# More borders in the side work, another order for the first pair of products, and side work that rests while operands are split

## The chip, the cores and the metric

The kernel runs on one core of a Trainium2 chip. The metric is device time in microseconds of one execution; the profile adds one profiled execution with its span from the first to the last instruction. Engines are named as the profile names them: PE (matrix products), PEld (its weight loads), DVE, ACT and POOL (elementwise work), SP (the queue that issues the DMAs).

## The reference

One step of a decoder layer for 1024 prompt tokens and 8 samples of 4 tokens (1056 token columns), width 1024, all in float32:

```python
sh1, sc1, g1, sh2, sc2, g2 = split(silu(c) @ w_ada + b_ada, 6)   # per sequence
h = ln(x) * (1 + sc1) + sh1
qm, km, vm, ig, fg, og, qa, ka, va, gm, ga = split(h @ w_in + b_in)
hm = ln(mlstm(qm, km, vm, ig, log_sigmoid(fg))) * norm_w * sigmoid(og)   # 4 heads, chunks of 128
ha = sliding_window_attention(qa, ka, va)                        # 16 heads, 4 kv heads, window 128
x = ln(ALPHA * x + g1 * ((sigmoid(gm) * (hm @ w_branch_m) + sigmoid(ga) * (ha @ w_branch_a)) @ w_out))
h2 = ln(x) * (1 + sc2) + sh2
x = ln(ALPHA * x + g2 * ((gelu(conv_a(h2 @ w_up)) * conv_b(h2 @ w_up)) @ w_down))
```

Outputs are x for prompt and samples and the new states: mLSTM matrix, normaliser and maximum, the last 128 keys and values, the last two columns before the convolution.

## The kernel before

**Products.** Each float32 operand is split in two parts of a shorter format (hi, a cast on ACT; lo, a subtraction on DVE) and a product is hi·hi + hi·lo + lo·hi: three matmuls for each 128-deep piece. `group` (lines 440 to 449) makes one 128-row block of a product for one of three column tiles (384, 384 and 288 columns, `TT`): eight pieces, 24 matmuls, in one of three PSUM banks `L`. `Stream` loads the weights of a block two blocks ahead and splits them one block ahead (`win.ahead_of`).

**Stages.** First the norm of x and four blocks for the branch gate (`direct(0)` to `direct(3)`). Then ten pairs of blocks in a form with seven half-size products instead of eight (`fast`, `Pair`, products numbered 1 to 7 at line 1445). Then 28 blocks and the gate rows for the heads (`direct`, line 1545). Then the branch stages: eight blocks of `w_branch_m` (line 1667), called BM0 to BM7 here, and eight of `w_branch_a` (line 1685), BA0 to BA7. Then `w_out`, the up and down products and the end.

**Side work.** The gate rows (`gate_rows`), the mLSTM heads (`mlstm`), the attention groups (`swa`) and the remaining modulation vectors (`ada_rest`) are Python generators in a queue `sides`. A `yield` is a border between two steps. `group` calls `pulse(nt / 800)` after each piece; `pulse` adds that times `rate[0]` to a counter and runs one step for each whole unit. So a block of three tiles is worth 8 · (0.48 + 0.48 + 0.36) = 10.56 units, a step comes each 1/rate units, and the order of all instructions on each engine is fixed when the program is built. `finish_sides` runs what is left with no products between. `mlstm` sets the rate to `RATE_M`, `swa` to `RATE_S`.

**Places that the change touches.**
- `fast`: `t1_split` (line 1354) splits the operands of product 5 on ACT and DVE before the first product. Products 1 and 2 read the same split weights `pa`; product 6 reads those of `ps[0]`, split in the last step of `first_pair` (`step(2)`, lines 1403 and 1404).
- `gate_rows` (line 642): exponentials on ACT, scans and elementwise work on DVE, in 13 steps.
- `mlstm` (line 802): 11 steps for the chunks, then the sample part. Copies into `C0T` (line 930), a border, products on them (line 937). Then `norm_apply` into `hs` (line 761 through line 979), a border, transposes of `hs`.
- `swa` (line 1043): two steps that split the queries (line 1064), then 13 steps of a software pipeline; its first step computes the biases `bg`, the scores (line 1184) and the sample scores (line 1086), a later one copies scores (lines 1189 and 1190).
- The last `direct` block (qa, block 7) sets the rate to 0, reads the finished heads back from DRAM (`raw_pieces`, line 1303) and splits them tile by tile into the operands of BM (`refill`, lines 1313 and 1314). The rate goes back to `RATE_S` at line 1639, ahead of BM0.
- BM7 reads the attention outputs back (16 pieces of 192 KB, later 8 of 144 KB), refills the operands, and puts `ada_rest` in the queue: a load of four tiles of 512 KB (line 231), three borders, 32 matmuls (line 241), and so on eight times.

Of the kernel before, what the change touches and what calls it, by code (L numbers as in the profile page):

```python
# [30 lines left out]
TT = [(0, 384), (384, 384), (768, 288)]  # L31
NSLOT = 43

RATE_G, RATE_M, RATE_S, RATE_A = 0.44, 0.54, 0.46, 0.46
RATES = [0.442, 0.395, 0.35, 0.45, 0.463, 0.495, 1.0, 0.7, 0.417]


# [67 lines left out]
def hybrid_step(ctx: ExitStack, tc: tile.TileContext, I, O):  # L105
# [48 lines left out]
    rate = [0.26]  # L154
# [487 lines left out]
    def gate_rows():  # L642
        fi, lf = rows_f["i"], rows_f["f"]
        na, rm, bb, Q, M, t5 = (slot(name="gr") for _ in range(6))
        r = slice(0, 4)
        V.memset(Q, 0.0)
        V.memset(rm[r], 1.0)
        V.memset(rm[r, 0:SEQ:128], 0.0)
        V.memset(rm[r, SEQ:TOK:4], 0.0)
        V.scalar_tensor_tensor(na[r], lf[r], -1.0, lf[r], op0=OP.mult, op1=OP.max)  # L650
        yield
        yield
        A.activation(na[r], na[r], AF.Exp, scale=-1.0)
        A.activation(na[r], na[r], AF.Ln, bias=1.0)
        yield
        V.scalar_tensor_tensor(lf[r], lf[r], 0.0, na[r], op0=OP.min, op1=OP.subtract)
        V.tensor_tensor_scan(bb[r], rm[r], lf[r], 0.0, op0=OP.mult, op1=OP.add)
        g = Q[r]
        V.tensor_tensor(g, fi[r], bb[r], op=OP.subtract)
        yield  # L660
        d0 = na
        V.memset(d0[r, :SEQ], 0.0)
        V.tensor_copy(d0[r, 128:SEQ:128], bb[r, 127:SEQ - 1:128])
        V.memset(d0[r, SEQ:], BIG)
        V.memset(d0[r, SEQ:TOK:4], -BIG)
        gs = t5[r, SEQ:]
        V.tensor_copy(gs, Q[r, SEQ:])
        V.tensor_tensor(gs[:, 0:32:4], gs[:, 0:32:4], m0, op=OP.max)
        V.tensor_tensor_scan(M[r, :SEQ], d0[r, :SEQ], Q[r, :SEQ], 0.0, op0=OP.add, op1=OP.max)
        V.tensor_tensor_scan(M[r, SEQ:], d0[r, SEQ:], gs, -BIG, op0=OP.min, op1=OP.max)  # L670
        mp = tiny([4, 16], "mp", 1)
        MT = tiny([4, 16], "MT", 1)
        bT = tiny([4, 16], "bT", 1)
        dec = tiny([4, 16], "dec", 1)
        V.tensor_copy(MT[:, 0:8], M[r, 127:SEQ:128])
        V.tensor_copy(MT[:, 8:16], M[r, SEQ + 3:TOK:4])
        V.tensor_copy(bT[:, 0:8], bb[r, 127:SEQ:128])
        V.tensor_copy(bT[:, 8:16], bb[r, SEQ + 3:TOK:4])
        V.tensor_tensor(mnew, bT, MT, op=OP.add)
        V.memset(mp[:, 0:1], 0.0)  # L680
        V.tensor_copy(mp[:, 1:8], mnew[:, 0:7])
        V.tensor_copy(mp[:, 8:16], m0)
        V.tensor_tensor(dec, mp, MT, op=OP.subtract)
        S.dma_start(mD, M[r])

        def bc(x):
            return (x[:, 0:8][:, :, None].to_broadcast([4, 8, 128]), x[:, 8:16][:, :, None].to_broadcast([4, 8, 4]))

        t = lf
        p8, s8 = bc(MT)  # L690
        V.tensor_tensor(chunks(t[r, :SEQ]), chunks(Q[r, :SEQ]), p8, op=OP.subtract)
        V.tensor_tensor(to3(t[r, SEQ:]), to3(Q[r, SEQ:]), s8, op=OP.subtract)
        t = fi
        p8, s8 = bc(mp)
        V.tensor_tensor(chunks(t[r, :SEQ]), p8, chunks(M[r, :SEQ]), op=OP.subtract)
        V.tensor_tensor(to3(t[r, SEQ:]), s8, to3(M[r, SEQ:]), op=OP.subtract)
        V.tensor_tensor(t5[r], bb[r], M[r], op=OP.add)
        for _ in range(4):
            yield
        A.activation(dec, dec, AF.Exp)  # L700
        S.dma_start(dD, dec)
        A.activation(Q[32:36], lf[r], AF.Exp)
        A.activation(Q[64:68], fi[r], AF.Exp)
        A.activation(Q[96:100], t5[r], AF.Exp, scale=-1.0)
        S.dma_start(aD, Q[64:68])
        S.dma_start(decb.rearrange("p a b -> p (a b)"), dap(dD, 0, [[0, 128], [1, 64]]))
        S.dma_start(O["p_m"].rearrange("a b c -> (a b) c").rearrange("a c -> c a"), mnew[:, 7:8])
        S.dma_start(O["s_m"].rearrange("a b c -> (a b) c").rearrange("a c -> c a"), mnew[:, 8:16])
        for _ in range(4):
            yield  # L710
        for i in range(8):
            transpose(pd(i), Q[:, i * 128:(i + 1) * 128])
        transpose(PE_[:32, :128], Q[:, SEQ:])
        for i in range(2):
            V.tensor_copy(colQ[:, 4 * i:4 * i + 4],
                          PD[i].rearrange("p (i q x) -> p i q x", i=4, q=4)[:, :, :, 0:4])
        V.tensor_copy(colQ[:32, 8], PE_[:32, :128].rearrange("p (q x) -> p q x", q=4)[:, :, 0:4])
        drop(fi, lf, na, rm, bb, Q, M, t5)
        yield
# [82 lines left out]
    def mlstm(h):  # L802
# [117 lines left out]
        for q4 in range(2):  # L920
            for half_ in range(2):
                p = ((PF, PG) if q4 else PD)[half_]
                for bi in range(2):
                    b = 4 * q4 + 2 * half_ + bi
                    for vb in range(2):
                        o = bi * 256 + vb * 128
                        transpose(p[:, o:o + 128], C0[vb][:, b * 128:(b + 1) * 128])
                eng = A.copy if half_ else V.tensor_copy
                eng(c0v[q4][:, 2 * half_:2 * half_ + 2, 0:256], p.rearrange("p (b x) -> p b x", b=2))
            V.tensor_copy(c0v[q4][:, :, 256:257], n0T.rearrange("p (b h) -> p b h", h=4)[:, 4 * q4:4 * q4 + 4, h:h + 1])  # L930
            if q4:
                go_ahead(h + 1)
            yield
        for r in range(2):
            for j in range(4):
                b = 4 * r + j
                T.matmul(PE_[32 * j:32 * j + 32, :257], qm[:, b, :], c0v[r][:, j, :], start=r == 0, stop=r == 1,
                         tile_position=(0, 32 * j))
# [38 lines left out]
        yield  # L977
        hs = tiny([32, 256], "hs", 1, "isb")
        norm_apply(hs, num[:, :256], nrm, 32)
        yield  # L980
        for i in range(2):
            transpose(PG[:, i * 32:(i + 1) * 32], hs[:, i * 128:(i + 1) * 128], 32)
# [60 lines left out]
    def swa(g):  # L1043
        rate[0] = RATE_S
        p, o = g // 2, g % 2
# [14 lines left out]
        for j in range(2):  # L1060
# [5 lines left out]
                G.tensor_copy(qs[me, :, 2 * j + hh, :], to3(zq[j][a, SEQ:]))  # L1066
            yield
        drop(*zq)
        bg = tiny([128, 4, 128], "bg", 1)
        for i in range(4):  # L1070
            V.tensor_scalar(bg[:, i, :], cst[:, C_DELTA:C_DELTA + 128], slope(4 * g + i), None, op0=OP.mult)
# [60 lines left out]
        for s in range(13):  # L1132
# [39 lines left out]
            n = s  # L1172
# [95 lines left out]
    def ada_rest():  # L1268
        todo = [(ca, cb, 256 * s) for ca, cb in ((3, 4), (2, 5)) for s in range(4)]
        w = ada_load(*todo[0])  # L1270
        for i, (ca, cb, f0) in enumerate(todo):
            for _ in range(3):
                yield
            ada_mm(w)
            if i + 1 < len(todo):
                w = ada_load(*todo[i + 1])
            sa = ada_copy()
            yield
            ada_sel(sa, f0)
            ada_put(ca, cb, f0)  # L1280
# [70 lines left out]
            V.tensor_tensor(t3_ops[kp][1], e[:, :, 1, :], t3_ops[kp][0].bitcast(F32), op=OP.subtract)  # L1351
            yield

    def t1_split():

        for kp in range(4):
            hi, lo = (quarters(t)[:, :, 1, :] for t in acts[2 * kp])
            x = quarters(hf[2 * kp])[:, :, 0, :]
            A.copy(hi, x)
            V.tensor_tensor(lo, x, hi.bitcast(F32), op=OP.subtract)  # L1360
        drop(hf[4], hf[6])

    def operand(p, kp, g):

# [114 lines left out]
    def fast(pairs, at_end):  # L1479

        prev = None
        t1_split()
        for n, pr in enumerate([*pairs, None]):
            nxt = pairs[n + 1] if n + 1 < len(pairs) else None
            for pos, p in enumerate((1, 3, 6, 2, 7, 4, 5)):
                who = prev if p == 3 else pr
                if who is not None:
                    for g in range(2):
# [7 lines left out]
                if pos == 0:  # L1496
                    if n:
                        pr.step(2)
                elif pos == 1:
                    pr.step(3)  # L1500
                    pr.step(4)
                elif pos == 2 and nxt is not None:
                    nxt.load()
                    if n in (2, 4):
                        kept_cache(n // 4)
                elif pos == 3:
                    drop(*pr.pa)
                elif pos == 4 and nxt is not None:
                    nxt.step(0)
                elif pos == 5:  # L1510
                    drop(pr.pq)
                    if nxt is not None:
                        nxt.step(1)
                elif pos == 6:
                    drop(*pr.ps[0])
# [120 lines left out]
        return t  # L1636

    nxt = gate_load("gm", 0)
    rate[0] = RATE_S
    mD2 = [dram.tile([128, TOK], F32, name=f"moutD{j}") for j in range(8)]  # L1640

    def m_out(j, t):
# [8 lines left out]
    for j in range(8):  # L1651
# [11 lines left out]
        for ti, (t0, nt) in enumerate(TT):  # L1663
            ps = lbank()
            if ti == (not j):
                win.ahead_of(BM + j)
            group(ps, win.parts[BM + j], acts, TT[ti])
            V.tensor_tensor(gt[:, t0:t0 + nt], ps[:, :nt], gt[:, t0:t0 + nt], op=OP.mult)
            if j == 7:
# [558 lines left out]
```

## Time and profile before

| | us |
|---|---|
| median of 3 runs (lowest, highest) | 2037.14 (2032.62, 2042.41) |
| the profiled execution | 2039.19 |
| its span | 2037.3 |
| PE busy | 1950.2 |
| DVE busy | 1116.8 |
| ACT busy | 738.2 |
| mean granted PE clock | 0.981 |

PE is busy almost all the time, so the time between its matmuls and the time at a granted clock of 0.5 are what there is to look for. A row of the waits names who waited, for whom, the sum, the count and the longest. A timeline row has start, duration, engine, line, operation and, in brackets, the idle time before it with what ended it.

### The profile page before, as it was taken

To read this page: it belongs to the slowest core of one execution; us is meant where nothing else is said; L and a number is where in the kernel's file an instruction comes from. 1 tells how busy PE (TensorE), PEld (TensorE's weight loads), DVE (VectorE), ACT (ScalarE), POOL (GpSimd) and SP (SyncE) were. 2 spreads that over 40 slices of the span, in tenths; PEclk is the share of its full clock that TensorE was granted. 3 is DMA by queue.
4 is the path that set the end of the run, shared out by engine and by line. 5 is a ranking of instruction groups with operands and counts; after the bars stand their busy time and mean duration, and the time that the engine had idled before them with its cause. 6 is when DMAs were issued, how large, how long until landed. Compare 5 with 4: busy or idle time off the path is not lost. (4 is left out here: it accounts for less than half of the span.)

```text
span 2037.3 us, 32186 instructions
## 1 busy us (share of the span) xinstructions
PE 1950.2 (96%) x12837; PEld 1851.3 (91%) x12837; DVE 1116.8 (55%) x2374; ACT 738.2 (36%) x1530; POOL 303.8 (15%) x592
## 2 busy tenths in 40 slices
PE   6999999998999999899799999999999999999996
PEld 4999998988898889888689999999999999999995
DVE  5666665555655462654334355474545454646579
ACT  5431224443443563545211345443222222223331
POOL 2000000422440321123000153100000000000007
PEclk9999999999999999899899999999999999999998
DMA  9224343464343213333884323111211111111533
GB/s 292 85 91 149 96 128 67 148 171 135 92 123 95 64 43 100 116 117 106 284 292 146 94 93 120 46 34 47 62 33 48 47 47 48 47 40 48 195 127 127
DMA packets 222942, 216.03 MB, mean 106 GB/s; under 512 B 9745, under 2 KB 199873, under 8 KB 222761
## 3 DMA queue, kind: packets, MB, share of 16 engines
q1 hardware_dynamic: 222013, 213.38, 34.1%
q8 instruction: 100, 1.64, 0.3%
q10 hardware_dynamic: 780, 0.61, 0.1%
q14 instruction: 49, 0.40, 0.1%
HBM read 164.12 MB, written 51.87 MB: 106 GB/s over the span
## 5 line engine op out<-in xcount | busy, mean ns | idle before, releaser
L448 PE MATMUL L<-mhi,whi 128*128 128x384 f32 (+1 forms) x1248 | 408.5, 327 | 4.8 <-DVE r L1807 3.0
L448 PE MATMUL L<-mhi,wlo 128*128 128x384 f32 (+1 forms) x1248 | 404.0, 324 | 0.0
L448 PE MATMUL L<-mlo,whi 128*128 128x384 f32 (+1 forms) x1248 | 403.5, 323 | 0.1
L448 PE MATMUL L<-hhi,whi 128*128 128x384 f32 (+1 forms) x1120 | 375.8, 336 | 0.1
L448 PE MATMUL L<-hhi,wlo 128*128 128x384 f32 (+1 forms) x1120 | 367.1, 328 | 2.6 <-DVE wlo L426 2.6
L448 PE MATMUL L<-hlo,whi 128*128 128x384 f32 (+1 forms) x1120 | 366.8, 328 | 0.0
L426 DVE TENSOR_TENSOR wlo<-wraw,whi 128x1024 fp32r<-128x1024 f32 (+1 forms) x128 | 150.1, 1173 | 328.6 <-ACT whi L422 328.1
L448 PEld LDWEIGHTS L<-mhi,whi 128*128 128x128 f32 x1248 | 235.7, 189 | 6.6 <-DVE r L1807 3.3
L448 PEld LDWEIGHTS L<-mlo,whi 128*128 128x128 f32 x1248 | 235.7, 189 | 0.3 <-DVE mlo L1780 0.3
L448 PEld LDWEIGHTS L<-mhi,wlo 128*128 128x128 f32 x1248 | 235.3, 189 | 0.0
L448 PEld LDWEIGHTS L<-hhi,whi 128*128 128x128 f32 x1120 | 215.5, 192 | 6.7 <-issue 4.8
L448 PEld LDWEIGHTS L<-hhi,wlo 128*128 128x128 f32 x1120 | 215.1, 192 | 2.9 <-DVE wlo L426 2.9
L448 PEld LDWEIGHTS L<-hlo,whi 128*128 128x128 f32 x1120 | 215.8, 193 | 0.4
L1852 ACT ACTIVATE u<-L,vT 128x384 f32<-128x384 f32 (+1 forms) x132 | 71.9, 546 | 379.7 <-PE L L448 379.6
L448 PE MATMUL L<-ahi,whi 128*128 128x384 f32 (+1 forms) x432 | 139.6, 323 | 0.0
L448 PE MATMUL L<-alo,whi 128*128 128x384 f32 (+1 forms) x432 | 139.3, 323 | 0.0
L448 PE MATMUL L<-ahi,wlo 128*128 128x384 f32 (+1 forms) x432 | 139.3, 322 | 0.0
L422 ACT CAST whi<-wraw 128x1024 fp32r<-128x1024 f32 (+1 forms) x128 | 128.2, 1003 | 28.4 <-DMA wraw<-in_w_up 19.6
L1865 DVE SCALAR_TENSOR_TENSOR y<-u,vT,y 128x1023 f32<-128x1023 f32 (+3 forms) x92 | 113.7, 1235 | 2.5
L1875 POOL COPY ucol<-u 128x2 f32<-128x2 f32 x44 | 10.4, 236 | 631.2 <-ACT u L1852 631.2
L2021 DVE TENSOR_TENSOR facc<-L,facc 128x384 f32<-128x384 f32 (+1 forms) x120 | 62.7, 522 | 58.4 <-PE L L448 58.3
L448 PEld LDWEIGHTS L<-ahi,whi 128*128 128x128 f32 x432 | 81.2, 188 | 0.0
(579 smaller groups left out, 3586.5 us busy)
## 6 DMA issues: line engine op xcount, KB each, us to landing
wada<-in_w_ada SPq DMA_DIRECT2D x44, 512.0 KB
wraw<-in_w_up SPq DMA_DIRECT2D x44, 512.0 KB
wraw<-in_w_in SPq DMA_DIRECT2D x32, 512.0 KB
fraw<-in_w_in SPq DMA_DIRECT2D x20, 512.0 KB
wraw<-in_w_down SPq DMA_DIRECT2D x24, 384.0 KB
vD<-fdst SPq DMA_DIRECT2D x8, 528.0 KB
ogD<-fdst SPq DMA_DIRECT2D x8, 528.0 KB
v<-vD SPq DMA_DIRECT2D x8, 528.0 KB
```

The costliest lines, as they stand in the source:

```text
L422: A.copy(hi[:, :n], t[:, :n])
L426: V.tensor_tensor(lo[:, :n], t[:, :n], hi[:, :n].bitcast(F32), op=OP.subtract)
L448: T.matmul(ps[:, :nt], x[:, c], y[:, t0:t0 + nt], start=i == 0, stop=i == last)
L1852: A.activation(u[:, t0:t0 + n], ps[:, :n], AF.Identity, bias=b)
L1865: V.scalar_tensor_tensor(y[:, f:b], u[:, f - d:b - d], w[i], y[:, f:b], op0=OP.mult, op1=OP.add)
L1875: G.tensor_copy(aux["ucol"][:, c, 0:2], u[:, SEQ - 2:SEQ])
L2021: V.tensor_tensor(fx, ps[:, :nt], fx, op=OP.add)
```

## The change

Six borders (`yield`) are added and one is taken out in `gate_rows`, `mlstm` and `swa`, and five in a row stand before the first product of `ada_rest`; the four rates go up by 2 to 4%. The first pair's products come in the order 1, 2, 6, 7, 4, 5 instead of 1, 6, 2, 7, 4, 5 (product 3 belongs to the pair before and the first pair has none), and its `t1_split` is cut in three parts. The rate goes back to `RATE_S` one tile later, after BM0's first tile.

```diff
-RATE_G, RATE_M, RATE_S, RATE_A = 0.44, 0.54, 0.46, 0.46
+RATE_G, RATE_M, RATE_S, RATE_A = 0.46, 0.56, 0.475, 0.47
...
         V.tensor_tensor_scan(bb[r], rm[r], lf[r], 0.0, op0=OP.mult, op1=OP.add)
+        yield
...
         V.tensor_tensor(gs[:, 0:32:4], gs[:, 0:32:4], m0, op=OP.max)
+        yield
         V.tensor_tensor_scan(M[r, :SEQ], d0[r, :SEQ], Q[r, :SEQ], 0.0, op0=OP.add, op1=OP.max)
...
+        yield
         t = lf
...
-        for _ in range(4):
+        for _ in range(3):
             yield
         A.activation(dec, dec, AF.Exp)
...
             if q4:
                 go_ahead(h + 1)
             yield
+        yield
         for r in range(2):
...
         norm_apply(hs, num[:, :256], nrm, 32)
+        yield
         yield
...
         drop(*zq)
+        yield
         bg = tiny([128, 4, 128], "bg", 1)
...
         w = ada_load(*todo[0])
+        for _ in range(5):
+            yield
...
-    def t1_split():
+    def t1_split(kps):
 
-        for kp in range(4):
+        for kp in kps:
...
-        drop(hf[4], hf[6])
+            if kp > 1:
+                drop(hf[2 * kp])
...
-        t1_split()
+        t1_split([0])
...
-            for pos, p in enumerate((1, 3, 6, 2, 7, 4, 5)):
+            for pos, p in enumerate((1, 3, 6, 2, 7, 4, 5) if n else (1, 3, 2, 6, 7, 4, 5)):
...
                 if pos == 0:
                     if n:
                         pr.step(2)
+                    else:
+                        t1_split([1])
                 elif pos == 1:
                     pr.step(3)
                     pr.step(4)
+                    if not n:
+                        t1_split([2, 3])
...
     nxt = gate_load("gm", 0)
-    rate[0] = RATE_S
...
             if ti == (not j):
                 win.ahead_of(BM + j)
+                if not j:
+                    rate[0] = RATE_S
```

## Rows read from the trace of the kernel before

**Rows 1.** The page: busy time of PE, and the granted clock of PE in 40 slices of the span, in tenths.

```profile
PE 1950.2 (96%) x12837; PEld 1851.3 (91%) x12837; DVE 1116.8 (55%) x2374; ACT 738.2 (36%) x1530; POOL 303.8 (15%) x592
...
PEclk9999999999999999899899999999999999999998
```

**Rows 2.** The waits of PE over the whole span: who waited for whom, us in total, times, longest.

```profile
PE PE L241 <- DMA wada<-in_w_ada: 11.8, 4, 10.4
PE PD L1184 <- DVE scr L1190: 8.1, 3, 6.0
PE PE L937 <- DVE C0T L930: 6.2, 5, 1.9
PE PD L1445 <- ACT fhi L1403: 5.5, 1, 5.5
PE PG L197 <- ACT hs L761: 4.8, 4, 1.7
...
PE L L448 <- DVE wlo L426: 2.6, 1, 2.6
PE PD L1184 <- DVE q L1064: 2.4, 3, 0.8
...
PE PE L832 <- DVE wx L843: 2.3, 3, 1.5
```

**Rows 3.** Stretches around those waits: start and end, length, busy time of PE, PEld, DVE, ACT and POOL with their instructions, then the granted clock of PE, the DMA share and GB/s.

```profile
98.00:110.00 12.00, 5.92 (x29) 5.40 (x28) 10.79 (x17) 7.17 (x12) 0.00 (x0) 0.72 0.26 83
348.00:353.00 5.00, 4.81 (x19) 4.81 (x20) 1.36 (x2) 1.55 (x3) 0.00 (x0) 0.66 0.84 47
419.00:428.00 9.00, 6.82 (x38) 4.73 (x37) 7.68 (x20) 3.48 (x6) 0.12 (x1) 0.81 0.81 221
...
551.00:558.00 7.00, 5.89 (x32) 4.12 (x33) 6.58 (x18) 1.54 (x3) 0.00 (x0) 0.76 0.79 244
613.00:620.00 7.00, 7.00 (x51) 4.98 (x50) 3.04 (x12) 0.96 (x2) 0.00 (x0) 1.00 0.60 72
646.00:656.00 10.00, 9.07 (x46) 8.68 (x45) 5.29 (x19) 2.57 (x12) 0.00 (x0) 0.66 0.21 52
719.00:728.00 9.00, 8.09 (x47) 7.61 (x45) 5.49 (x20) 2.90 (x13) 0.00 (x0) 0.81 0.23 60
813.00:824.00 11.00, 10.25 (x54) 10.00 (x54) 5.41 (x19) 2.53 (x5) 0.00 (x0) 0.69 0.24 73
843.00:851.00 8.00, 6.49 (x25) 6.49 (x26) 5.18 (x26) 4.83 (x22) 1.04 (x1) 0.57 0.50 157
904.00:913.00 9.00, 8.89 (x52) 8.66 (x51) 5.23 (x19) 2.13 (x11) 0.00 (x0) 0.81 0.21 64
985.00:1001.00 16.00, 5.15 (x25) 1.94 (x26) 5.32 (x11) 4.36 (x9) 0.00 (x0) 0.68 1.08 361
```

**Rows 4.** Timeline of the first pair: on PE the first matmul of product 6 and the first of product 7, on ACT and DVE the splits of product 6's weights.

```profile
104.15 0.59 PE L1445 MATMUL PD<-thi,fhi 128*128 128x264 f32 x1 [5.48 <-ACT fhi L1403]
105.55 0.59 PE L1445 MATMUL PD<-thi,flo 128*128 128x264 f32 x1 [0.59 <-DVE flo L1404]
...
113.16 0.28 PE L1445 MATMUL L<-th,fhi 128*128 128x264 f32 x1
...
103.06 1.03 ACT L1403 CAST fhi<-fsum 128x1024 fp32r<-128x1024 f32 x1
...
108.49 1.22 DVE L1404 TENSOR_TENSOR flo<-fsum,fhi 128x1024 fp32r<-128x1024 f32 x1
```

**Rows 5.** Timeline around the gate rows: the cast of a block's weights on ACT, the second scan and the subtraction for the same weights on DVE.

```profile
334.16 1.04 ACT L422 CAST whi<-wraw 128x1024 fp32r<-128x1024 f32 x1
...
338.50 0.91 DVE L662 MEMSET gr<- 4x1024 f32 x1 [0.16 <-issue]
...
346.93 1.21 DVE L426 TENSOR_TENSOR wlo<-wraw,whi 128x1024 fp32r<-128x1024 f32 x1
```

**Rows 6.** Timeline of PE where the fourth attention group begins: the sample scores.

```profile
906.06 1.96 PE L1086 MATMUL PG<-qs,kcT 64*128 64x16 f32 x16
```

**Rows 7.** Timeline of BM0's begin: its first matmul and the wait on PE, on ACT the last cast of the refill, on DVE the copies of scores that PE waits for.

```profile
834.12 0.34 PE L448 MATMUL L<-hhi,whi 128*128 128x384 f32 x1
...
844.51 0.58 PE L1184 MATMUL PD<-khi,q 128*128 128x256 f32 x1 [6.01 <-DVE scr L1190]
...
841.65 0.43 ACT L1313 CAST hhi<-raw 128x288 fp32r<-128x288 f32 x1 [1.06 <-DMA raw<-hD]
...
844.01 0.77 DVE L1190 COPY_PREDICATED scr<-cst,PD 128x256 f32<-128x256 int32 x2 [1.44 <-ACT scr L1189]
```

**Rows 8.** BM7: the evacuations of BM6's last two tiles and BM7's first on DVE (each begins as its tile ends), the wait on PE, SP's issues, and the casts of the third tile's refill.

```profile
972.85 0.56 DVE L1668 TENSOR_TENSOR gate<-L,gate 128x384 f32<-128x384 f32 x1 [3.64 <-PE L L448]
975.99 0.46 DVE L1668 TENSOR_TENSOR gate<-L,gate 128x288 f32<-128x288 f32 x1 [2.58 <-PE L L448]
980.18 0.56 DVE L1668 TENSOR_TENSOR gate<-L,gate 128x384 f32<-128x384 f32 x1 [2.60 <-PE L L448]
...
995.53 1.06 PE L241 MATMUL PE<-wada,cT 128*32 128x256 f32 x2 [10.41 <-DMA wada<-in_w_ada]
...
992.98 7.35 SPq L1303 DMA_DIRECT2D raw<-haD  x8
...
1002.55 2.77 ACT L1313 CAST hhi<-raw 128x288 fp32r<-128x288 f32 x8
```

## The prediction, made before the changed kernel ran

> **What bounds the kernel now.** I read the page first, then the waits of PE, then the granted clock around each wait, then timelines there. PE is busy 1950.2 of 2037.3 us, and the clock row is nine tenths or more in most slices and lower in a few [rows 1]. So the kernel is a stream of matmuls with holes, and a change in the side work can only pay by closing holes. The waits name them [rows 2]: the modulation weights (11.8 us, 10.4 of it at once), scores waiting for a copy (8.1, 6.0 at once), the state copies C0T (6.2 in five waits), the first pair's split weights (5.5 on ACT, and 0.6 on DVE [rows 4]), hs (4.8 in four), one weight split (2.6) and the query split (2.4 in three). The edits' places are these, 38.5 us of idle time (10.4 + 6.0 + 6.2 + 6.1 + 4.8 + 2.6 + 2.4). A second loss stands beside them: the granted clock falls to the 1.2 GHz level after many of these waits. (1 - clock) times the stretch [rows 3] gives 3.4 us for the first pair, 1.7 after the weight split, 1.7 for the first and the third head each (I take three heads, 5.1), 3.4, 1.7, 3.4 and 1.7 at the begins of the four attention groups (10.2), 3.4 at BM0 and 5.1 at BM7: 28.9 us, of which what lies in an idle moment counts with the wait, not here.
>
> **The change part by part.** A step comes each 1/rate units. BM6's third tile and BM7's first end at 975.99 and 980.18 [rows 8], 4.2 us for the 3.84 units of a wide tile, so a unit is 1.09 us and a step at the old head rate 1 / 0.54 · 1.09 = 2.0 us. An empty border therefore gives the waited engine 2 us more, and PE fills them with `group` matmuls that it has to do anyway.
>
> *A, first pair.* Idle 5.48 + 0.59 before and in product 6 [rows 4]. Product 2 reads weights that product 1 has used, so it runs in the hole: a product pair is 24 matmuls, and from 105.55 on two pairs end by 113.16, some at half clock. At full clock a pair takes about 3.0 us (the two of product 2 stand between product 6's end near 110.2 and 113.16). So PE would be busy until 98.67 + 3.0 = 101.7 and then still wait for the weights: the cast begins at 103.06 after a chain of DVE work that no edit touches. Product 6 then ends near 108.5 at full clock, or 109.7 if the remaining 2.4 us of idle still cost some clock, and product 7 needs the DVE split that ends at 109.7 now and about 1.3 us earlier once two of four `t1_split` subtractions are behind it. Against 113.16 that is 3.5 us saved (bounds 1.5, and 9.5 if no wait is left and all clock comes back).
>
> *B, gate rows.* The weights' cast was done at 335.2, the subtraction came at 346.93 because the gate rows' long step, from 338.50, stands before it in DVE's order [rows 5]. The counter stands at its cap of 0.9 with an empty queue, so steps fall 0.48 units after the first block begins and each 1 / 0.46 = 2.17 units after that; with the added border the step with the memset and copies is the sixth, at 11.3, behind the next block's `ahead_of` at 10.56. The subtraction then goes ahead of it, some 8 us earlier than now. Saved 2.6 + 1.7 = 4.3 (bounds 0, if another long step takes its place, and 4.3).
>
> *C, C0T.* One border is 2 us against five waits in the first three heads, 2.1 us per head: 6.2 - 0.2. The clock: the fourth head has no such wait, and its stretch stands at 1.00 [rows 3], so without the wait the products themselves keep the clock; 5.1 back. Saved 11.1 (bounds 6.0, 11.3).
>
> *D, hs.* Longest wait 1.7 [rows 2], under one border: 4.8 (bounds 2.4, 4.8).
>
> *E, queries.* 2.4 of idle go. The clock is another matter: the fourth group has almost no wait there, and its stretch still reads 0.81 [rows 3], beside the 16 sample products of 1.96 us with 16 columns each [rows 6], which stay. So I leave 1.7 us of loss at each of four begins, 6.8 of 10.2, and take 3.5 back: 5.9 (bounds 2.4, 12.6).
>
> *F, resting.* BM0 began at 834.12, two attention steps fell in its first tile, and the second's scores waited 6.01 us for a copy that queued on ACT behind the refill, whose last cast began at 841.65 on a DMA [rows 7]. With rate 0 and the extra border, the group's first scores come just before the last qa block, the next after four pieces of BM0's second tile (834.12 + 4.2 + 2.1 = 840.4), the third one tile end later, about 843.5 with their own matmuls. ACT has the refill until 842.1; then come the weights' cast of BM1 (1.04 [rows 5]), which is emitted at that tile too, what lies between refill and copies now (until 844.01, 1.9 us), and the copies of 0.77: through at 845.8. I leave 2.4 us of wait, since 845.8 - 843.5 = 2.3. Saved 3.6, and 2.0 of the clock's 3.4: 5.6 (bounds 2.0, 9.4).
>
> *G, ada.* PE stood 10.41 us for wada [rows 8]. Five borders move the 32 matmuls from BM7's third tile to BA0's third tile, about 5 / 0.47 · 1.09 = 11.6 us later. But the hole isn't free: the DMA share is 1.08 there at 361 GB/s [rows 3], and in SP's order behind wada stand the eight pieces for BA0's third tile, issued until 1000.3 and cast from 1002.55 without a pause until 1005.3 [rows 8]. PE without the wait: BM7 begins at 976.0 and takes 11.5, two tiles of BA0 8.4, so it wants those operands at 995.9. They are bound by the transfers, not by PE, so the wait moves there; the first piece can't be in much before 1001. Of the clock's 5.1 about half lies in the idle time, 2.6 beside work. I take 5.5 us left of wait and 2.0 of clock: 10.4 + 2.6 - 5.5 - 2.0 = 5.5 saved (bounds 0, 13.0).
>
> *H, rates and phase.* Steps come 2 to 4% closer. The waits in this stretch that no border serves are wx 2.3 and the rest of scr 2.1 [rows 2], with smaller ones under them about 8 us together; I let them grow by half: 4.0 lost (bounds 8 lost, 1 gained). Step counts: the gate rows have 15 steps for 13, each head 20 for 18, each group 18 for 17, in all 177 for 163 before BM7. The last two groups can't begin before qa block 5 ends; from there to BM7 lie 10.56 + 6.72 + 6 · 10.56 = 80.6 units, at 0.475 38.3 steps for 36. So all ends 2 steps ahead of `finish_sides`, and `ada_rest` (37 steps of 44 that BM7 and BA hold) before `w_out` reads it.
>
> Sum: 3.5 + 4.3 + 11.1 + 4.8 + 5.9 + 5.6 + 5.5 - 4.0 = 36.7. The profiled execution took 2039.2, 2.0 above the median of 2037.1; from the median: 2000.
>
> A rule against C and D: the Trainium skill, "Perfetto Trace Analysis", section "Identifying Performance Opportunities", says that the same gap repeating on the engine that should be saturated can mean that no buffer is free for the next tile. By it the repeated waits would stay, 15.9 us less saved, 2016. The trace speaks against it: the waits are on the engines that write what PE reads (C0T by DVE, hs by ACT [rows 2]), not on a reader of PE's banks.
>
> **The rivals.** (1) *The clock stays low.* Waits shrink, but the small products hold the granted clock down as in the fourth group: without the clock's part of B, C, E and F (1.7 + 5.1 + 3.5 + 2.0 = 12.3) 2013. For it: 0.81 with no wait in 904 to 913. Against: 1.00 in 613 to 620 [rows 3]. (2) *The two operand refills hold PE anyway* (F and G nothing, A 1.5): 36.7 - 13.1 = 24, 2013. For it: DMA share 1.08. Against: at BM0 PE has a tile and a half more to do first. (3) *Everything closes*, refills too: uppers of A, E, F and G make 2000 - 24 = 1976. Against it the cast at 103.06 and the pieces until 1000.3. (4) *Slower: bare steps.* If the longer side work isn't through at `finish_sides`, each step left runs with no `group` matmuls beside it and PE waits out its chain: about 3 us (the chain that makes a C0T wait 2 us beside work, and its DVE part). It decides from 12 steps on (36.7 / 3), 16 for 0.5% slower, 2050; my count leaves 2 steps of room, so it needs a miscount by more than a group. (5) *The change doesn't do it:* the borders move each step into another tight place, gains and new waits cancel: 2034.
>
> **How the numbers follow.** Chances: forecast 0.58 (own range 1988 to 2009), (1) 0.15, (2) 0.12, (3) 0.05, (4) 0.03, (5) 0.03, the repeated gaps staying 0.04. What a measurement can tell from no change is about 0.5%, 10 us. Range 1985 to 2018: it takes in (1), (2) and the low ends of E and G together, and leaves out most of (3) to (5). Faster by over 0.5% (under 2027): all but (4), (5) and mixtures of (1) and (2), 0.90; within 0.5% 0.06; slower 0.04.
>
> **What would show it.** A: product 6 with a wait of some 2.5 us instead of 5.5. B, C, D: no wait on wlo, C0T, hs above 0.3 us, clock 1.00 there. E: no wait on q, but a clock below 1 at some of the four begins. F: a wait on scr of 1 to 4 us in BM0. G: no wait on wada of 10 us, and a new one on the refill (hhi or hlo) at BA0's third tile of about 5 us. It is wrong if that last wait is missing, if the clock's loss stays near 29 us, or if `finish_sides` shows matmuls of the groups alone.

## The result and the profile after

| | before | after |
|---|---|---|
| median of 4 runs each, us | 2037.92 | 2005.91 (2004.68 to 2007.6) |
| ratio, 95% interval | | 0.984 (0.982 to 0.987) |
| the profiled execution, us | 2039.19 | 2004.68 |
| its span, us | 2037.3 | 2002.6 |
| mean granted PE clock | 0.981 | 0.989 |

The changed kernel is 32.0 us faster by the medians, 34.7 by the profiled spans; the forecast was 2000, with 36.7 saved. The page of the kernel after, busy time and granted clock in tenths:

```profile
PE 1936.5 (97%) x12837; PEld 1838.5 (92%) x12837; DVE 1116.0 (56%) x2374; ACT 737.0 (37%) x1530; POOL 301.6 (15%) x592
...
PEclk9999999999999999999999999999999999999998
```

The same 12837 matmuls are busy for 13.7 us less than in [rows 1], which goes with the higher granted clock. The rest is idle time: span less PE busy was 87.1 us and is 66.1, 21.0 less. The waits of PE after, in the columns of [rows 2]:

```profile
PE PD L1190 <- DVE scr L1196: 6.4, 5, 2.8
PE PE L241 <- DMA wada<-in_w_ada: 5.9, 4, 4.2
PE L L448 <- ACT hhi L1321: 5.8, 1, 5.8
...
PE PE L1454 <- ACT fhi L1412: 2.5, 1, 2.5
...
PE PE L1454 <- DVE flo L1413: 0.9, 1, 0.9
PE L L448 <- DVE wlo L426: 0.6, 1, 0.6
PE PE L941 <- DVE C0T L933: 0.5, 2, 0.3
PE PG L197 <- ACT hs L764: 0.2, 1, 0.2
```

The waits on C0T, hs and wlo are all but gone, that on the query split is no longer listed, and the 10.4 us at once on wada has become a wait of 5.8 on `hhi`, the refill. The waits on copied scores (`scr`) are shorter, 2.8 at most, but still 6.4 in all for 8.1. (What is left on wada lies before 43 us, in the first modulation vectors.) The places of [rows 3] in the kernel after, in the same columns:

```profile
98.00:112.00 14.00, 10.57 (x63) 10.14 (x63) 11.33 (x18) 8.10 (x13) 0.00 (x0) 0.76 0.37 107
340.00:350.00 10.00, 10.00 (x65) 10.00 (x64) 7.45 (x17) 6.87 (x9) 0.00 (x0) 1.00 0.22 56
414.00:424.00 10.00, 9.50 (x60) 7.01 (x59) 8.54 (x20) 4.28 (x8) 1.37 (x2) 1.00 0.77 195
...
300.00:630.00 330.00, 322.72 (x2168) 301.31 (x2168) 186.13 (x542) 145.86 (x344) 99.19 (x216) 1.00 0.49 126
...
636.00:660.00 24.00, 22.09 (x133) 21.36 (x133) 15.15 (x66) 11.41 (x45) 2.08 (x2) 0.86 0.17 45
706.00:714.00 8.00, 8.00 (x56) 7.93 (x54) 7.46 (x14) 4.06 (x5) 0.00 (x0) 1.00 0.29 93
792.00:802.00 10.00, 10.00 (x68) 9.90 (x67) 4.68 (x15) 3.57 (x8) 0.00 (x0) 1.00 0.14 42
818.00:827.00 9.00, 5.94 (x32) 5.62 (x33) 7.08 (x30) 5.01 (x26) 1.04 (x1) 0.81 0.45 142
880.00:890.00 10.00, 10.00 (x74) 9.70 (x73) 7.72 (x25) 3.71 (x13) 0.00 (x0) 1.00 0.21 64
964.00:976.00 12.00, 6.19 (x38) 3.68 (x38) 4.84 (x11) 3.96 (x9) 0.00 (x0) 0.72 1.02 323
```

The clock is whole after the weight split (340), through all the heads (300 to 630), and at the begins of the second to fourth attention group (706, 792, 880). It still falls at the first pair, near the first group (636 to 660), at BM0 and in BA0. (1 - clock) times these four stretches is some 12 us, where the prediction counted 28.9 before. The timeline at these places, with the idle time and its releaser in brackets:

```profile
104.64 0.39 PE L1454 MATMUL PE<-thi,fhi 128*128 128x264 f32 x1 [2.54 <-ACT fhi L1412]
...
111.05 0.42 PE L1454 MATMUL L<-th,fhi 128*128 128x264 f32 x1
...
820.27 0.39 PE L1190 MATMUL PD<-khi,q 128*128 128x256 f32 x1 [2.81 <-DVE scr L1196]
...
945.00 0.46 DVE L1682 TENSOR_TENSOR gate<-L,gate 128x288 f32<-128x288 f32 x1 [2.59 <-PE L L448]
...
956.14 6.57 SPq L231 DMA_DIRECT2D wada<-in_w_ada  x4
...
962.76 7.38 SPq L1311 DMA_DIRECT2D raw<-haD  x8
...
970.26 3.01 ACT L1321 CAST hhi<-raw 128x288 fp32r<-128x288 f32 x8 [10.37 <-DMA raw<-haD]
...
970.75 0.61 PE L448 MATMUL L<-hhi,whi 128*128 128x288 f32 x1 [5.81 <-ACT hhi L1321]
```

The row at 111.05 is the first matmul of product 7. The cast that PE waits for in BA0 had itself waited 10.4 us for the DMA of the eight pieces.

The evacuation of BM6's last tile begins at 945.00 and was at 975.99 [rows 8]: 31.0 us are gained by then. Such a difference of one evacuation's begin in two traces is called its lead here. A lead is a gain only where both kernels have run the same side work by then. That is so at the ends of BM6 and BA7; up to BM6's end both have run 6402 matmuls (the first row is of the kernel before, the second of the kernel after):

```profile
0.00:975.99 975.99, 920.47 (x6402) 853.80 (x6403) 545.10 (x1505) 416.58 (x1027) 187.71 (x360) 0.98 0.39 116
...
0.00:945.00 945.00, 906.23 (x6402) 840.02 (x6403) 544.23 (x1504) 415.48 (x1027) 185.73 (x360) 0.99 0.41 120
```

| up to | lead after, us | of it idle time of PE | forecast |
|---|---|---|---|
| end of BM6 | 31.0 | 16.8 | A to F and H 31.2 |
| end of BA7 | 36.5 | 21.6 | with G 36.7 |
| end of the span | 34.7 | 21.0 | 36.7 |

So the sum holds within 1 us up to BA7, and only the last row has no term. The single terms can't be read from leads inside the heads. At the end of the heads (third tile of `va`, 603.21 before) the lead is 24.3 us, one tile earlier 28.2 and one later 21.3: at this tile the kernel before has run 4020 matmuls and the kernel after 3982, since the added borders put side work behind. Taken one by one the terms hold less well than the sum, as the runs show.

### The profile page after: what moved, and what is told of

It is laid out like the page before. It is cut to its first block, busy times and chain, and to the rows that moved or that the text cites. A ratio compares the mean times of both kernels' runs of the same rounds, so it can differ in the third digit from the quotient of the medians.

```text
span 2002.6 us, 32182 instructions
## 1 busy us (share of the span) xinstructions
PE 1936.5 (97%) x12837; PEld 1838.5 (92%) x12837; DVE 1116.0 (56%) x2374; ACT 737.0 (37%) x1530; POOL 301.6 (15%) x592
## 5 line engine op out<-in xcount | busy, mean ns | idle before, releaser
L448 PE MATMUL L<-hhi,wlo 128*128 128x384 f32 (+1 forms) x1120 | 362.7, 324 | 0.0
```

What stands on the lines that cost most here:

```text
L448: T.matmul(ps[:, :nt], x[:, c], y[:, t0:t0 + nt], start=i == 0, stop=i == last)
```

## The experiments

Times are medians; the interval is of the ratio to the kernel before on the same chip. "Later" and "earlier" are now against the kernel after, and at the ends of BM6 and BA7, where the side work done is the same. The kernel after has 0.982 to 0.987. Of the removals only that of the attention border (0.987 to 0.991) and that of the modulation borders (0.987 to 0.990) lie at or above its upper end; the other six are not told apart from it by the times. What is said of those rests on the waits that return, and on one execution each.

**One part undone at a time.** The pair's order:

```diff
-for pos, p in enumerate((1, 3, 6, 2, 7, 4, 5) if n else (1, 3, 2, 6, 7, 4, 5)):
+for pos, p in enumerate((1, 3, 6, 2, 7, 4, 5)):
```

> The changed kernel with the first pair's products in the old order (1, 6, 2, 7, 4, 5), the split of product 5's operands still cut in three. Theory (product 2 fills part of the hole before product 6's weights): PE waits 5.5 us before product 6 again instead of 2.5, and product 7 begins 2 to 3.5 us later; span 2005 to 2006. Rival (the cut of the operand split did it, since the split stood before the weights' work on ACT and DVE): the wait stays near 2.5 us and the span near 2002.6.

2004.88 us, 0.984 (0.982 to 0.987). The wait on `fhi` is 5.5 us again, product 7 starts 2.5 later and the end is 2.5 later in the profile, while the medians cannot tell the two apart. So product 2 fills part of the hole and is worth 2.5 us at product 7, not 3.5.

The border before C0T:

```diff
-        yield
         for r in range(2):
```

> The changed kernel without the border between the C0T copies and the products that read them (four steps fewer). Theory: waits of PE on C0T of about 6 us in all come back (0.5 now), with a granted clock of 0.5 after three of them, 5 us; span 2010 to 2014. Rival (the rates and the other borders have moved the steps, so the border is no longer needed): waits on C0T under 2 us, span within 2 us of 2002.6.

2007.5 us, 0.986 (0.984 to 0.987). Its waits on C0T, and the stretches around them in the first and the third head:

```profile
PE PE L940 <- DVE C0T L933: 5.4, 6, 2.4
```

```profile
410.00:424.00 14.00, 11.38 (x65) 8.90 (x64) 10.71 (x29) 5.35 (x9) 1.37 (x2) 0.88 0.70 164
540.00:552.00 12.00, 10.45 (x61) 8.03 (x61) 8.96 (x26) 3.91 (x8) 1.42 (x2) 0.86 0.56 92
```

The idle time returns almost whole, 4.9 us more than after, and the clock falls at two heads for 1.7 us each ((1 - clock) times the stretch). That is 8.3 us for C's 11.1, which had the clock at three heads. At the end of BM6 the kernel is 6.0 us later, at BA7 7.3 and at the end 4.9. (The lead at the end of the heads is 12.4 us, but by then this kernel has run more side work than after.)

The resting of the side work (the rate set before BM0 again):

```diff
+    rate[0] = RATE_S
     mD2 = [dram.tile([128, TOK], F32, name=f"moutD{j}") for j in range(8)]
...
-                if not j:
-                    rate[0] = RATE_S
```

> The changed kernel with the attention rate set ahead of BM0's first tile again. Theory (ACT is behind the refill until its last pieces land): two steps fall in BM0's first tile, PE waits about 6 us on copied scores there instead of 2.8 + 0.8, and a lower clock follows; BM6 ends 3 to 5 us later. Rival (the extra border before the first scores alone has cured it, since those scores now lie before the last qa block in both): the wait stays under 3.6 us, span within 1 us of 2002.6.

2006.78 us, 0.985 (0.984 to 0.987); profiled span 6.3 longer. The wait on `scr` is 4.5 at once instead of 2.8, and BM6 ends 6.4 later. But 3.3 of that is there before BM0 begins, at the last qa tile, where the edit has done nothing yet; it is clock lost at begins of groups (last section). So the wait speaks for F, and its 5.6 us is not shown.

The borders before the modulation products:

```diff
-        for _ in range(5):
-            yield
```

> The changed kernel without the five borders in front of the first modulation product. Theory (transfers bind this stretch, so the borders only moved the wait to the refill of BA0's third tile, 5.8 us there, and saved the rest): a wait of about 10.5 us on wada in BM7, none on the refill, BA0 ends 4 to 6 us later, span 2007 to 2009. Rival (the wait just moved and nothing was saved): span within 1.5 us of 2002.6. Second rival (the whole 10.4 us and its clock were saved and the refill wait has another cause): span 2013 or more with the refill wait still there.

2012.69 us, 0.988 (0.987 to 0.990). The wait on PE in BM7:

```profile
965.75 1.03 PE L241 MATMUL PE<-wada,cT 128*32 128x256 f32 x2 [11.21 <-DMA wada<-in_w_ada]
```

The wait on `hhi` is gone and 11.2 on wada is back, 5.4 more than the 5.8; BA7 is 6.3 later and the end 4.6, 6.8 by the medians. G's 5.5 is right, and so is this reading of it: the borders replaced one wait by another half as long.

The four old rates:

```diff
-RATE_G, RATE_M, RATE_S, RATE_A = 0.46, 0.56, 0.475, 0.47
+RATE_G, RATE_M, RATE_S, RATE_A = 0.44, 0.54, 0.46, 0.46
```

> The changed kernel with the four rates of before (0.44, 0.54, 0.46, 0.46). Theory (the side work still ends about one step before or after finish_sides, and steps a little farther apart cost nothing): span within 3 us of 2002.6, one step at most left bare. Rival (the rates carry the change: without them the 14 added borders push the side work out of room, and steps run bare): several steps without group matmuls before BM7, span 2010 or more. Second rival (closer steps cost about 4 us as the prediction's term H says): span near 1999.

2003.32 us, 0.982 (0.981 to 0.984), span 0.1 longer. It is 6.6 us earlier than after at the end of BM6 and 4.0 at BA7, and level at the end. So the closer steps do cost 4.0 to 6.6 us on the way, near H's 4.0; what takes that back after BA7 is told below. Even at the old rates the side work ends before `finish_sides`, but barely: the last attention matmul begins at 936.99, and BM6's last tile ends at 938.40.

The gate rows' borders:

```diff
-        yield
...
-        for _ in range(3):
+        for _ in range(4):
             yield
```

> The changed kernel with the gate rows' steps as before (13 instead of 15). Theory: the wait of about 2.6 us on a weight split (wlo) after qa/k/q blocks' start near 347 us comes back with a lower clock, 4 us by the end of the first q blocks; span 2005 to 2007. Rival (the raised rate alone moved the long step behind the weight split): no such wait, span within 1 us of 2002.6.

2004.31 us, 0.983 (0.981 to 0.984). (The diff shows one of the three borders taken out.) The wait and the clock come back where they were:

```profile
PE L L448 <- DVE wlo L426: 2.6, 1, 2.6
```

```profile
340.00:352.00 12.00, 9.42 (x51) 9.10 (x50) 6.92 (x17) 5.82 (x8) 0.00 (x0) 0.86 0.55 64
```

The wait of 2.6 and (1 - clock) times the stretch, 1.7, are B's 4.3, so B is right in its place. At the end of BM6 this kernel is 0.3 earlier all the same, at the end 0.4. Whether B is worth anything there is not shown: over the span PE is idle for 69.6 us, 3.5 more than after, but at a higher granted clock (0.991 for 0.989).

The border before the first attention step:

```diff
         drop(*zq)
-        yield
```

> The changed kernel without the border between the query splits and the first scores. Theory: waits on the query split of about 2.4 us in all come back, and at some of the four begins of the groups the granted clock reads 0.5 for longer than now (now once, near 641): 4 to 8 us more by BM6's end. Rival (the clock falls for the sample products themselves, so only the idle time counts): 2 to 3 us more.

2018.08 us, 0.989 (0.987 to 0.991): this one undoes about a third of the gain. Its waits, and the begins of the first, second and fourth group:

```profile
PE PD L1189 <- DVE q L1069: 3.5, 4, 0.9
...
PE PD L1189 <- DVE scr L1195: 8.0, 4, 5.4
```

```profile
640.00:648.00 8.00, 8.00 (x47) 7.77 (x47) 3.89 (x23) 3.22 (x13) 0.00 (x0) 0.79 0.01 2
705.00:718.00 13.00, 12.15 (x61) 11.62 (x61) 8.69 (x30) 5.00 (x15) 0.00 (x0) 0.74 0.28 82
...
886.00:896.00 10.00, 10.00 (x61) 9.69 (x61) 6.28 (x31) 2.76 (x12) 0.00 (x0) 0.83 0.01 2
```

The clock is low at the begins again, which the kernel after has only near the first (its 706, 792 and 880 rows read 1.00). That this is the border's doing is not shown: the kernel with the later load below has the border, and falls of the same size at three begins (last section). What does follow is the idle time, 43.8 us up to BM6's end for 38.8 in the kernel after: the waits on the query split are back, and the wait on `scr` at BM0 is 5.4 at once, for 2.8. (That it is another step that now meets BM0, the group being one step shorter, is argued and not tried.) BM6 ends 9.7 later; another 5.0 comes after BA7.

The second border behind hs:

```diff
         norm_apply(hs, num[:, :256], nrm, 32)
-        yield
         yield
```

> The changed kernel without the second border between norm_apply of the samples and the transposes of hs. Theory: waits on hs of 4 to 5 us in four pieces come back, no clock is lost; span 2006 to 2008. Rival (other steps take up the room): waits on hs under 1.5 us, span within 1.5 us of 2002.6.

2009.14 us, 0.985 (0.983 to 0.987). Four waits on hs are back, 7.2 us in all and 2.7 at most, with a clock of 0.5 after the longest, at 494. BM6 ends 7.0 later and the span 6.8, though the medians are only 3.2 apart. In this trace D's 4.8 is low: the waits are longer than they were in the kernel before, and D had no term for the clock.

The eight removals add up to some 39 us in profiled spans, for 34.7 of the whole change, but to 19.4 by the medians, for 32.0: the profiled execution of the kernel after was the fastest of its four. So these sums don't say how far the parts overlap or need each other.

**One part alone.** The border of the attention groups in the kernel before:

```diff
         drop(*zq)
+        yield
```

> The kernel before with one edit alone, the border between the query splits and the first scores. Theory (that border takes the begin of each group out of the low clock and moves the third group's second step, so it is the largest part, 12 us as its removal showed): 10 to 14 us faster than before, 2023 to 2027. Rival (it pays only together with the other edits, or the 14.7 us of its removal were partly a chance of phase in later stages): 3 to 7 us faster, 2030 to 2034.

2037.12 us, 1.000 (0.999 to 1.001). It runs 8.1 us ahead of the kernel before at the end of BM6 and 7.0 at BA7, and 1.1 at the end. Waits of this run after BA7, and the stretch from `w_out` on:

```profile
PE L L448 <- ACT u L1853: 3.0, 2, 1.9
PE L L448 <- DVE r L1808: 2.6, 1, 2.6
PE L L448 <- ACT r L1806: 2.4, 2, 2.1
```

```profile
1120.00:1275.00 155.00, 146.62 (x893) 142.62 (x893) 73.70 (x123) 68.48 (x97) 49.27 (x63) 0.97 0.31 97
```

Neither theory had this: the gain of the attention stretch is there, and the `w_out` and up stages take 5.9 us of it back. In the kernel before the waits on ACT's `r` and `u` after BA7 are 0.6 and 1.2 us, here 2.4 and 3.0, in places that no edit touches.

**What takes gains back after BA7.** From BA7's last evacuation to the end, in the kernels before and after, with the old rates, and with the attention border alone:

```profile
1121.72:2037.30 915.58, 894.89 (x5501) 877.52 (x5499) 509.90 (x748) 288.86 (x440) 116.07 (x232) 0.99 0.23 72
...
1085.19:2002.60 917.41, 896.08 (x5501) 878.49 (x5499) 509.82 (x748) 288.59 (x440) 115.83 (x232) 0.99 0.23 72
...
1081.20:2002.70 921.50, 897.32 (x5501) 878.96 (x5499) 509.69 (x748) 289.23 (x440) 116.15 (x232) 0.99 0.23 72
...
1114.77:2036.20 921.43, 897.36 (x5501) 879.02 (x5499) 509.83 (x748) 289.03 (x440) 115.80 (x232) 0.99 0.23 72
```

With the attention border removed the stretch takes 922.5 us; in the other nine runs it takes 915.0 to 917.0. The three long ones have one and the same order of instructions on PE, ACT, DVE and POOL there, and ACT's order in it (a few casts and evacuations stand a place elsewhere) is found in no other run. All three have the same waits, 2.4 us on `r` and 3.0 on `u`. So the loss of 4 to 6 us goes with this order and not with the single execution, and edits far ahead of the stretch can bring it about. The 1.8 us by which the kernel after is slower here than the kernel before are another thing: PE, ACT and POOL have the same order in both, and the five kernels with all orders as after spread from 916.1 to 917.4 us.

**What holds the refill.** In the order of SP above, 2 MB of wada go out at 956.14, ahead of the 1.2 MB for BA0's third tile at 962.76. The load is put two borders later, behind them:

```diff
+        for _ in range(2):
+            yield
         w = ada_load(*todo[0])
-        for _ in range(5):
+        for _ in range(7):
             yield
```

> The changed kernel with two borders in front of the first modulation load and seven behind it, so that SP issues the eight pieces for BA0's third tile ahead of wada, and the first modulation product comes in BA1. Theory (the 5.8 us wait at BA0's third tile is the DMA queue's order, wada's 2 MB being ahead of 1.2 MB that PE needs first): that wait falls to 2 us or less, no wait on wada over 1 us, BA3 ends about 5 us earlier, span 1995 to 1998. Rival (the transfers bind the stretch whatever their order): the wait only moves, to wada or to the next weights, span 2001 or more.

1998.89 us (1993.37 to 2001.17), 0.981 (0.979 to 0.983): faster than both kernels, with a profiled span of 1996.8 as the theory had it. SP's issues, and all of PE's waits from 940 to 1000:

```profile
958.18 7.97 SPq L1313 DMA_DIRECT2D raw<-haD  x8
...
966.21 2.31 SPq L231 DMA_DIRECT2D wada<-in_w_ada  x4
```

```profile
PE L L448 <- DVE gate L1703: 1.6, 1, 1.6
```

With the order turned round the cast of the eight pieces begins at 966.27 for 970.26, the wait on `hhi` is gone, and the products don't wait for wada either. Between the ends of BM6 and BA7 6.5 us are gained. So the hole in G was the order of the transfers, not their amount.

The same with the rate set one tile later in BM0, at 0.495:

```diff
-                if not j:
-                    rate[0] = RATE_S
+            if ti == 2 and not j:
+                rate[0] = 0.495
```

> e9_ada_later with the side work resting through BM0's second tile too, and 0.495 for the rest of the third group. Theory (the waits of 2.8 and 0.8 us on copied scores in BM0 stand behind the refill on ACT): these waits fall under 1 us together, and the lower clock near 822 goes, 3 to 5 us less than e9; the last group ends a step before finish_sides. Rival (denser steps and the later end give it back): within 1.5 us of e9, or above it.

1998.19 us (1991.35 to 1999.63), 0.980 (0.978 to 0.982): not told apart from the run before. The wait on `scr` in BM0 is 2.4 us at once, not under 1, so a rest of one more tile isn't what F lacked. The lower clock near 822 is gone, as the theory had it:

```profile
818.00:827.00 9.00, 6.65 (x44) 6.32 (x43) 6.92 (x33) 5.88 (x26) 1.79 (x2) 1.00 0.39 123
```

The split of product 5's operands in one piece again, with the new order:

```diff
-        t1_split([0])
+        t1_split(range(4))
```

> The changed kernel with product 5's operands split as a whole ahead of product 1 again (new order of products kept). Theory (the cut brings product 7's weights forward): product 7 begins 1 to 2 us later than now. Rival (product 7's weights are early enough either way): no difference over 0.5 us there.

2006.76 us, 0.985 (0.983 to 0.986) (the two later calls are left out). The waits before product 6 are 2.54 and 0.89 as in after, and product 7 begins at 109.38, earlier than the 111.05 of after and not later. Cutting `t1_split` brought nothing; the order alone did A.

## Why the prediction was right

The time, 2005.9, lies in the range and in the forecast's own range, 5.9 above the forecast. The mechanism is the one forecast: borders let `group` matmuls fill the waits, and idle time (21.0 us) and a higher granted clock (13.7 us) share the gain. That the sum came out so near is in part luck, since errors of single terms cancel: up to BM6's end C measures 6.0 us for 11.1, and E and D 9.7 and 7.0 for 5.9 and 4.8, each from one execution. Point by point:

- *A* foresaw 2.4 us of wait and 2.5 was left. Product 7 begins 2.1 us earlier than before, and 2.5 later without the new order, for 3.5. The wait left still brought the low clock (0.76 in the first row of the stretches), and that size was off. That `t1_split` would help product 7 fell with the uncut run.
- *B* was right in its place (2.6 to none, clock 1.00), *C* in its wait (6.2 to 0.5) and high in its clock (3.4 for 5.1). Both took a local gain for one at the end: undone alone, B gives 0.4 back and C costs 4.9 in the profiles, and the medians show neither.
- *D* closed its wait (4.8 to 0.2); undone it costs 6.8 in the profile and 3.2 by the medians.
- *E* is the term that was most mis-sized. "I leave 1.7 us of loss at each of four begins": the 880 row reads 1.00 beside the same sample products that I held for the cause at 0.81. Here only the first begin lost clock, though another execution of the same instructions lost it at the other three (last section), so the products are not shown to be the cause. Undone, the part costs 9.7 us up to BM6, and 12.2 at the end by the medians, about 5 of them by the order after BA7. Alone in the old kernel it gains 8.1 up to BM6, and that order takes most of it back.
- *F* foresaw 2.4 us of wait left and 2.8 came at once, as late next on `scr`.
- *G* foresaw the new wait at BA0's third tile, 5.5 us on the refill: 5.8, gain 5.5 by the leads. It took the transfers for the bound, and the later load shows that their order was.
- *H* was put as 4.0 lost to closer steps; the old rates are 6.6 us ahead at BM6 and 4.0 at BA7. They end level, as their order after BA7 is the long one. For what the order there costs, 4 to 6 us in three of the runs, no term was set.

Of the rivals, the clock staying low (1) fell: its loss at these places went from 28.9 to some 12 us. (2) held for half of G only; (3) was partly to be had by another edit, as the later load shows; bare steps (4) did not come (the last attention matmul begins 8.5 us before BM6's end), and the gains were not cancelled (5). The Trainium skill ("Perfetto Trace Analysis", "Identifying Performance Opportunities") says that the same gap repeating on the engine that should be saturated can mean that there is no room for the next tile. The repeated gaps here were not of that kind: they closed with an empty border and no buffer more, C0T 6.2 to 0.5 us, hs 4.8 to 0.2. Which of ACT's few displaced instructions after BA7 makes the long order was not tried; it stays open.

## What to carry to other kernels

Where PE waits a microsecond or two for an engine that writes its operand, put other matmuls between the two: it pays for the wait, and again where the granted clock fell behind it. Where PE waits on transfers while the DMA engines are full, look at the order in the issuing queue before moving the reader. Price such edits at the end of the span as well as in their place, since in an order fixed beforehand a gain in one stage shifts all that follows and can be lost there; and compare two kernels only at points where both have done the same work.

## What the hardware showed

The clock's falls are not a matter of the instructions alone. The kernel with the later load has the instructions of the kernel after, in the same order, up to BM7. Its stretches at the begins of the second to fourth attention group:

```profile
705.00:720.00 15.00, 15.00 (x92) 14.70 (x91) 10.21 (x35) 5.55 (x16) 0.00 (x0) 0.89 0.22 71
790.00:800.00 10.00, 10.00 (x61) 9.90 (x61) 4.63 (x18) 1.70 (x3) 0.00 (x0) 0.83 0.14 42
...
880.00:890.00 10.00, 10.00 (x66) 9.90 (x65) 6.75 (x21) 3.03 (x12) 0.00 (x0) 0.84 0.17 52
```

and two of the kernel after for the same lengths (its 880 row stands above, at 1.00):

```profile
705.00:720.00 15.00, 15.00 (x100) 14.70 (x100) 11.85 (x34) 7.67 (x18) 0.00 (x0) 1.00 0.22 71
790.00:800.00 10.00, 10.00 (x72) 9.90 (x71) 5.74 (x19) 2.14 (x4) 0.00 (x0) 1.00 0.24 77
```

PE is busy throughout in all six, at 0.83 to 0.89 in one execution and at 1.00 in the other: (1 - clock) times the length is 1.6 to 1.7 us each. So one profile is no proof of a loss of this size: two executions of the same instructions can differ by some 5 us of clock at these three places. I had read the 0.81 of 904 to 913 [rows 3] as a property of the products there.
